# A float32 transformer block pair: activation transposes through DVE and a DRAM exchange in place of DVE blocks and PE

## The chip, the core and the metric

The kernel runs on one NeuronCore of one Trainium2 chip. The core has a matrix engine (PE), a vector engine (DVE), a scalar engine (ACT), a general engine (POOL) and a queue engine (SP) that here only issues DMA transfers. Each engine works through its own list of instructions in order and waits on semaphores for the others. Sixteen DMA engines move data between DRAM and the on-chip memory of 128 partitions; PE writes to a separate accumulator memory (PSUM), which DVE and ACT can read.

The metric is the device time of one execution in microseconds (us), the median of several runs. Lower is better.

## What is computed

Two transformer blocks over 256 tokens of width 2048, all in float32. Each ends in a gated FFN of hidden width 5632; these two FFNs are what the change touches most.

```python
def conv_ffn(h, w_up, conv_w, conv_b, w_down):          # block 1
    up = h @ w_up                                        # (256, 2048) @ (2048, 11264)
    padded = jnp.pad(up, ((0, 0), (CONV_WIDTH - 1, 0), (0, 0)))
    y = conv_b + conv_w[0] * padded[:, 0:seq]
    for tap in range(1, CONV_WIDTH):                     # three taps along the tokens
        y = y + conv_w[tap] * padded[:, tap:tap + seq]
    gate, val = jnp.split(y, 2, axis=-1)
    return (jax.nn.silu(gate) * val) @ w_down

def second_block(...):
    ...                                                  # two mixers, concatenated, @ w_out
    x = x + (jax.nn.silu(h2 @ w_gate) * (h2 @ w_up)) @ w_down
```

Ahead of its FFN, block 1 has a 16-head causal attention with forget gates, and block 2 has a gated linear attention (4 heads) beside a dilated attention (8 heads). Queries and keys are RMS-normalised by head in the two attentions; each block normalises its input by row, once before the mixer and once before the FFN.

## The kernel before

**Products.** All large products go through one routine, `gemm`. It makes an output of 256 tokens by 512 columns from activation tiles that have the contraction on their partitions ("turned" activations) and from weight blocks of 512 by 512 (1 MB, `raw`). To keep float32 accuracy on PE, ACT rounds each weight to a high part `wh` (line 105) and DVE takes the remainder `wl` (line 111); the activations are split in the same way, and PE adds three products (lines 118 to 120). A *unit* is half a weight block: 12 matmuls on one pair `wh`, `wl`. A gemm over 2048 rows has 8 units. The whole program has 784 units: first 12 gemms for q, k, v, then 4 (attention out), 22 of 8 units (first FFN, up), 4 of 22 units (first FFN, down), 12 (block 2 in), 4 (block 2 out), 22 (second FFN, gate and up), 4 of 22 units (second FFN, down).

**What sets the order.** The program is written in one fixed order, and each engine takes its own instructions from it in that order. Before the matmuls of unit u, `split_to(u + LEAD)` with LEAD = 4 writes out the split of unit u+4; there are 5 pairs of `wh`, `wl` (NSPL), so the split of unit u+4 can begin when PE has finished unit u-1. `dma_to` issues the load of a 1 MB block on SP, two blocks ahead of the split that reads it; there are 3 buffers (NRAW), so a load waits until DVE has split the block three before it. The work between the products (what a gemm's output needs) is written as Python generators. `pump()` runs each of them to its next `yield` after every unit but the last one of a gemm, so a `yield` puts what follows one unit later in every engine's list.

```python
for kg in kgs:
    while ready is not None and not ready(kg):
        pump()
    for half in range(2):
        split_to(u + LEAD)
        ...                       # 12 matmuls
        if n == tot:
            start_fast(evac(acc))
        else:
            pump()
```

**Turning activations.** A product leaves tokens on the partitions; the next product needs the contraction there. `flip` (line 296) does it on DVE with 16 transposes of 32 partitions by 256 elements, two to a pump, so that a flip spreads over 8 pumps; each instruction transposes its 32 by 32 blocks and moves them to another group of partitions. `transposes` (line 281) and line 656 do it on PE against an identity, into PSUM.

- `plain` flips q and k of head groups 0 to 2 of block 1, of both groups of the dilated attention, and of the linear attention. `head_norm` comes first (not in the linear attention): ACT squares, DVE sums, POOL makes the factor and multiplies. `attention` waits in Python until `kf` is there; its step s2 then puts the score matmuls `sc` into PE's list.
- `resid` flips three of the four column blocks of each residual.
- `conv_evac` serves the 22 gemms of the first FFN's up stage, pairs j = 0 to 10 of gate (part 0) and value (part 1). For j below PE_CONV = 8 it flips on DVE (tile `flip`); then ACT makes the current token's tap with the bias into `y` (line 664) and the two older taps into `taps` (line 667), POOL adds them (line 671). For j = 8 to 10 PE transposes (line 656, 4 to a group, 48 in all) and DVE adds the taps from PSUM. Part 0 ends with silu on ACT; in part 1 POOL multiplies by it (line 692), and ACT and DVE split the result into `g` for the down product.
- `up_evac` flips 10 of the 11 blocks of the second FFN on DVE and turns the last one with 8 transposes on PE.

Tiles between stages come from 33 slots that are given out in turn (`alloc`, `free`).

Of the kernel before, what the change touches and what calls it, by code (L numbers as in the profile page):

```python
# [40 lines left out]
PE_CONV = 8  # L41
# [3 lines left out]
def fox_gla_dilated_kernel(  # L45
# [29 lines left out]
    sidep = ctx.enter_context(tc.tile_pool(name="side", bufs=4, space=bass.MemoryType.PSUM))  # L75
    dramp = ctx.enter_context(tc.tile_pool(name="scratch", bufs=1, space=bass.MemoryType.DRAM))
# [23 lines left out]
    def col(c, n=1):  # L100
        return cols[:, c:c + n]
# [198 lines left out]
    def split_flipped(y, dst, gains):  # L300
        for half in range(2):
            d = dst[half]
            if gains is None:
                sl = slice(half * 2, half * 2 + 2)
                hi_of(d[:, :, 0], y[:, sl])
                lo_of(d[:, :, 1], y[:, sl], d[:, :, 0])
            else:
                for kk in range(2):
                    kt = half * 2 + kk
                    hi_of(d[:, kk, 0], y[:, kt], gains(kt))  # L310
                    lo_of(d[:, kk, 1], y[:, kt], d[:, kk, 0], gains(kt))

    def resid(cb, ss, tt, gcol, rname, done):
        def evac(acc):
# [4 lines left out]
            if cb < KG - 1:  # L319
                sumsq(ss, cb, h[cb])  # L320
                y = alloc([4, S], F32, "flip")
                yield from flip(h[cb], y)
                d = new_t(2, rname)
                split_flipped(y, d, gains)
                free(y)
# [37 lines left out]
    def plain(name, box, key, r, norm=False, flipped=False, gain=None):  # L363
        def evac(acc):
# [112 lines left out]
    def run_all():  # L477
# [156 lines left out]
        def conv_evac(j, part, keep):  # L634
            cb = part * JF + j

            def evac(acc):
                y = alloc([4, S], F32, "y")
                on_pe = j >= PE_CONV
                u_ = y.rearrange("p a c -> p (a c)").rearrange("p (t c) -> p t c", t=2)  # L640
                for t in range(2):
                    if not on_pe:
                        act.activation(out=u_[:, t], in_=acc[t], func=AF.Copy, scale=rows["r2"][:, t:t + 1])
                        continue
                    act.activation(out=y[:, t::2], in_=acc[t].rearrange("p (a c) -> p a c", a=2), func=AF.Copy,
                                   scale=rows["r2"][:, t:t + 1])
                yield
                if not on_pe:
                    f = alloc([4, S], F32, "flip")
                    yield from flip(u_, f)  # L650
                for half in range(2):
                    if on_pe:
                        ps = side([2, S], "up")
                        for kk in range(2):
                            for t in range(2):
                                pe.transpose(ps[:, kk, t * P:(t + 1) * P], y[:, half * 2 + t, kk * P:(kk + 1) * P],
                                             ident)
                    else:
                        ps = f[:, half * 2:half * 2 + 2]
                    if not on_pe:  # L660
                        tp = alloc([2, 2, S], F32, "taps")
                        for kk in range(2):
                            ch = cb * 4 + half * 2 + kk
                            act.activation(out=y[:, half * 2 + kk], in_=ps[:, kk], func=AF.Identity,  # L664
                                           scale=col(C_CW + 176 + ch), bias=col(C_CB + ch))
                            for d in (1, 2):
                                act.activation(out=tp[:, d - 1, kk, 0:S - d], in_=ps[:, kk, 0:S - d], func=AF.Copy,  # L667
                                               scale=col(C_CW + 176 - 88 * d + ch))
                        for d in (1, 2):
                            yy = y[:, half * 2:half * 2 + 2, d:S]  # L670
                            pool.tensor_tensor(out=yy, in0=yy, in1=tp[:, d - 1, :, 0:S - d], op=ALU.add)  # L671
                        free(tp)
                        yield
                        continue
                    for kk in range(2):
                        ch = cb * 4 + half * 2 + kk
                        yy = y[:, half * 2 + kk]
                        act.activation(out=yy, in_=ps[:, kk], func=AF.Identity, scale=col(C_CW + 176 + ch),
                                       bias=col(C_CB + ch))
# [5 lines left out]
                if not on_pe:  # L685
                    free(f)
# [375 lines left out]
```

## Time and profile before

| | |
|---|---|
| median of 3 runs | 2244.41 us (2244.35 to 2244.52) |
| the profiled execution, its own time | 2244.25 us |
| span of its instructions | 2242.5 us |
| PE busy | 2229.8 us, 99% |
| DVE busy | 1494.0 us, 67% |
| ACT busy | 1146.8 us, 51% |
| POOL busy | 259.7 us, 12% |
| DMA queue of SP, share of the 16 engines | 52.5%, 417.59 MB |

The span runs from the first to the last instruction; 1.75 us of the execution's time lie outside it. PE's busy time is the union of its matmuls, whose ends are modelled: a matmul is shown with 0.39 us though the next one starts 0.227 us after it. What PE loses is therefore read from the distance between starts and from its idle time, and not from the busy share alone.

### The profile page before, as it was taken

To read this page: it belongs to the slowest core of one execution; us is meant where nothing else is said; L and a number is where in the kernel's file an instruction comes from. 1 tells how busy PE (TensorE), PEld (TensorE's weight loads), DVE (VectorE), ACT (ScalarE), POOL (GpSimd) and SP (SyncE) were. 2 spreads that over 40 slices of the span, in tenths; PEclk is the share of its full clock that TensorE was granted. 3 is DMA by queue.
4 is the path that set the end of the run, shared out by engine and by line. 5 is a ranking of instruction groups with operands and counts; after the bars stand their busy time and mean duration, and the time that the engine had idled before them with its cause. 6 is when DMAs were issued, how large, how long until landed. Compare 5 with 4: busy or idle time off the path is not lost.

```text
span 2242.5 us, 25956 instructions
## 1 busy us (share of the span) xinstructions
PE 2229.8 (99%) x10004; PEld 1834.3 (82%) x10004; DVE 1494.0 (67%) x2012; ACT 1146.8 (51%) x1522; POOL 259.7 (12%) x210
## 2 busy tenths in 40 slices
PE   9999999999999999999999999999999999999999
PEld 7888888888888878888887887888888888888887
DVE  5877668777787776556666974586666666664443
ACT  6545554577667665444455544544444444443332
POOL 0323020033433310000111100000000000000000
PEclk9999999999999999999999999999999999999999
DMA  7654445545455554555554544555555555555553
GB/s 297 225 184 166 177 154 201 186 175 205 169 203 178 197 192 172 204 190 198 214 188 151 188 169 141 178 189 190 200 192 189 198 195 188 195 194 202 199 206 112
DMA packets 62189, 423.11 MB, mean 189 GB/s; under 512 B 6992, under 2 KB 7904, under 8 KB 12272
## 3 DMA queue, kind: packets, MB, share of 16 engines
q1 hardware_dynamic: 60272, 417.59, 52.5%
q0 software_dynamic: 928, 3.20, 0.4%
q8 instruction: 78, 1.28, 0.2%
q10 hardware_dynamic: 864, 0.66, 0.1%
q14 instruction: 47, 0.39, 0.0%
HBM read 419.30 MB, written 2.11 MB: 188 GB/s over the span
## 4 chain that ended last, share of the span: by engine, by line
PE 87%; DVE 5%; POOL 4%; ACT 2%; issue 1%; DMA 0%; ACTq 0%; DVEq 0%; SPq 0%
PE acc L118 28%; PE acc L119 28%; PE acc L120 28%; POOL y L671 3%; DVE wl L111 3%; DVE flip L296 1%; POOL y L692 1%; ACT taps L667 1%; ACT wh L105 0%; PE sc L413 0%; DMA xr<-in_x_t_dram 0%; PE pt L439 0%; PE nar L544 0%; ACT y L664 0%; DVE g L111 0%
## 5 line engine op out<-in xcount | busy, mean ns | idle before, releaser
L111 DVE TENSOR_TENSOR wl<-raw,wh 128x1024 fp32r<-128x1024 f32 (+1 forms) x786 | 973.8, 1243 | 598.6 <-ACT wh L105 593.9
L105 ACT CAST wh<-raw 128x1024 fp32r<-128x1024 f32 (+1 forms) x786 | 816.0, 1048 | 741.6 <-PE acc L120 726.7
L118 PE MATMUL acc<-wh,r 128*128 128x512 f32 x1792 | 703.1, 392 | 0.4 <-ACT wh L105 0.4
L119 PE MATMUL acc<-wl,r 128*128 128x512 f32 x1792 | 698.4, 390 | 4.1 <-DVE wl L111 4.1
L120 PE MATMUL acc<-wh,r 128*128 128x512 f32 x1792 | 697.9, 389 | 0.0
L119 PEld LDWEIGHTS acc<-wl,r 128*128 128x128 f32 x1792 | 336.6, 188 | 75.7 <-DVE wl L111 7.4
L118 PEld LDWEIGHTS acc<-wh,r 128*128 128x128 f32 x1792 | 336.5, 188 | 72.2 <-issue 2.5
L120 PEld LDWEIGHTS acc<-wh,r 128*128 128x128 f32 x1792 | 336.4, 188 | 70.2
L118 PE MATMUL acc<-wh,g 128*128 128x512 f32 x704 | 274.1, 389 | 0.0
L120 PE MATMUL acc<-wh,g 128*128 128x512 f32 x704 | 273.9, 389 | 0.0
L119 PE MATMUL acc<-wl,g 128*128 128x512 f32 x704 | 273.9, 389 | 0.0
L118 PE MATMUL acc<-wh,x 128*128 128x512 f32 x384 | 155.5, 405 | 0.2 <-ACT wh L105 0.2
L118 PEld LDWEIGHTS acc<-wh,g 128*128 128x128 f32 x704 | 132.2, 188 | 27.5
L119 PEld LDWEIGHTS acc<-wl,g 128*128 128x128 f32 x704 | 132.2, 188 | 27.3
L120 PEld LDWEIGHTS acc<-wh,g 128*128 128x128 f32 x704 | 132.1, 188 | 27.3
L119 PE MATMUL acc<-wl,x 128*128 128x512 f32 x384 | 149.8, 390 | 0.8 <-DVE wl L111 0.8
L120 PE MATMUL acc<-wh,x 128*128 128x512 f32 x384 | 150.0, 391 | 0.0
L671 POOL TENSOR_TENSOR y<-y,taps 128x510 f32<-128x510 f32 x64 | 106.4, 1662 | 253.5 <-ACT taps L667 250.1
L296 DVE STREAM_TRANSPOSE flip<-y 32x256 f32<-32x256 f32 x256 | 111.7, 436 | 5.6
L119 PEld LDWEIGHTS acc<-wl,x 128*128 128x128 f32 x384 | 72.2, 188 | 15.5 <-DVE wl L111 1.3
L120 PEld LDWEIGHTS acc<-wh,x 128*128 128x128 f32 x384 | 72.1, 188 | 15.6
L118 PEld LDWEIGHTS acc<-wh,x 128*128 128x128 f32 x384 | 72.2, 188 | 15.1 <-ACT wh L105 0.6
(206 smaller groups left out, 1611.8 us busy)
## 6 DMA issues: line engine op xcount, KB each, us to landing
raw<-in_w_dram SPq DMA_DIRECT2D x301, 1024.0 KB, 4.8
raw<-in_w7g_dram SPq DMA_DIRECT2D x44, 1024.0 KB, 4.8
raw<-in_w7u_dram SPq DMA_DIRECT2D x44, 1024.0 KB, 4.8
raw<-in_w_dram SPq DMA_DIRECT2D x4, 512.0 KB, 7.9
h<-in_x_dram SPq DMA_DIRECT2D x4, 512.0 KB, 9.5
ckb<-cum_dram POOLq DMA_DIRECT2D x4, 512.0 KB, 8.5
out_dram<-h SPq DMA_DIRECT2D x7, 256.0 KB, 2.2
xr<-in_x_t_dram SPq DMA_DIRECT2D x3, 512.0 KB, 8.0
```

The costliest lines, as they stand in the source:

```text
L105: act.copy(out_, in_)
L111: dve.tensor_tensor(out=out_, in0=in_, in1=hi.bitcast(F32), op=ALU.subtract)
L118: pe.matmul(out_, xh, wh, start=first, stop=False)
L119: pe.matmul(out_, xh, wl, start=False, stop=False)
L120: pe.matmul(out_, xl, wh, start=False, stop=last)
L296: dve.transpose(out=dv[32 * j:32 * j + 32, :, :, 32 * i:32 * i + 32], in_=sv[32 * i:32 * i + 32, :, :, j])
L667: act.activation(out=tp[:, d - 1, kk, 0:S - d], in_=ps[:, kk, 0:S - d], func=AF.Copy, scale=col(C_CW + 176 - 88 * d + ch))
L671: pool.tensor_tensor(out=yy, in0=yy, in1=tp[:, d - 1, :, 0:S - d], op=ALU.add)
L692: pool.tensor_tensor(out=y, in0=y, in1=sg, op=ALU.mult)
```

## The change

1. `flip` is now two DVE transposes of all 128 partitions by 512 elements (every 32 by 32 block is transposed where it stands, into a new tile `turn`), then a yield, then four DMA writes of 32 partitions each into a DRAM tile `way`, a yield, one DMA read of `way` back with the blocks at their final partitions, and two more yields. All five transfers are issued on SP. The read's target is the source tile itself (`into`) except in `resid`. What comes back has its tokens in four pieces by 32 for every 128 columns.
2. `ordered` puts the tokens in order: 4 copies on ACT of 128 by 256 (with the gain, where there is one). `split_flipped` uses it when there are gains, and otherwise splits straight from the pieces, 128 by 256 at a time.
3. `conv_evac` uses this for all 22 gemms: PE_CONV and the PE transposes of line 656 are gone. ACT makes the current tap from `n`, DVE adds the two older ones (8 instructions of 128 by 255 or 254), and DVE does the product with silu. POOL has no part in it.
4. `up_evac` uses it for the last block too, in place of 8 PE transposes.
5. A DRAM pool of 4 `way` tiles is added.

```diff
-    def flip(src, dst):
-        sv = src.rearrange("p t (k q c) -> p t k q c", q=4, c=32)
-        dv = dst.rearrange("p k (t r) -> p t k r", t=2)
+    def flip(src, into=None):
+        turn = alloc([4, S], F32, "turn")
+        sv = src.rearrange("p t (k q c) -> p t q k c", q=4, c=32)
+        qv = turn.rearrange("p q (k t r) -> p t q k r", t=2, r=32)
+        for t in range(2):
+            dve.transpose(out=qv[:, t], in_=sv[:, t])
+        yield
+        way = ways.tile([P, 4, S], F32, tag="way", name="way")
         for i in range(4):
-            for j in range(4):
-                dve.transpose(out=dv[32 * j:32 * j + 32, :, :, 32 * i:32 * i + 32], in_=sv[32 * i:32 * i + 32, :, :, j])
-                if j % 2:
-                    yield
+            nc.sync.dma_start(out=way[:, i].rearrange("(j c) e -> c j e", c=32), in_=turn[32 * i:32 * i + 32])
+        yield
+        held = alloc([4, S], F32, "flip") if into is None else into
+        f = held.rearrange("p a c -> p (a c)").rearrange("p (i e) -> p i e", i=4)
+        nc.sync.dma_start(out=f, in_=way)
+        yield
+        yield
+        free(turn)
+        return f.rearrange("p i (k t r) -> p k t i r", k=4, t=2), held
+
+    def ordered(f, name, scale=lambda kt: 1.0):
+        y = alloc([4, S], F32, name)
+        for kt in range(4):
+            act.activation(out=grid(y[:, kt]), in_=f[:, kt], func=AF.Copy, scale=scale(kt))
+        return y
...
@@ plain
-            y = alloc([4, S], F32, name + "f")
-            yield from flip(t_, y)
-            free(t_)
-            if gain is not None:
-                act.activation(out=y, in_=y, func=AF.Copy, scale=gain)
-            box[key + "f"] = y
+            f, held = yield from flip(t_, t_)
+            box[key + "f"] = ordered(f, name + "f", lambda kt: 1.0 if gain is None else gain)
+            free(held)
@@ conv_evac
+                u_ = alloc([2, 512], F32, "u")
+                for t in range(2):
+                    act.activation(out=u_[:, t], in_=acc[t], func=AF.Copy, scale=rows["r2"][:, t:t + 1])
+                yield
+                f, held = yield from flip(u_, u_)
+                n = ordered(f, "n")
+                free(held)
+                yield
                 y = alloc([4, S], F32, "y")
-                on_pe = j >= PE_CONV
...
+                for kt in range(4):
+                    ch = cb * 4 + kt
+                    act.activation(out=y[:, kt], in_=n[:, kt], func=AF.Identity, scale=col(C_CW + 176 + ch),
+                                   bias=col(C_CB + ch))
+                for kt in range(4):
+                    ch, yy = cb * 4 + kt, y[:, kt]
+                    for d in (1, 2):
+                        dve.scalar_tensor_tensor(out=yy[:, d:S], in0=n[:, kt, 0:S - d],
+                                                 scalar=col(C_CW + 176 - 88 * d + ch), in1=yy[:, d:S],
+                                                 op0=ALU.mult, op1=ALU.add)
+                    if kt == 1:
                         yield
...
-                pool.tensor_tensor(out=y, in0=y, in1=sg, op=ALU.mult)
+                dve.tensor_tensor(out=y, in0=y, in1=sg, op=ALU.mult)
@@ up_evac
-                if j < JF - 1:
-                    y = alloc([4, S], F32, "flip")
-                    yield from flip(t_, y)
-                    d = new_t(2, "g")
-                    split_flipped(y, d, None)
-                    free(y)
-                else:
-                    d = new_t(2, "g")
-                    transposes(t_, d, None)
+                f, held = yield from flip(t_, t_)
+                d = new_t(2, "g")
+                split_flipped(f, d, None)
+                free(held)
```

How the lists of three engines change. **SP**, from the early loads on, before (`raw` is a 1 MB weight block, `h` and `const` are loaded once):

```order
L154 DMA raw<-in_w_dram 128x2048
L163 DMA h_294<-in_x_dram 128x2x512
L154 DMA raw<-in_w_dram 128x2048
L159 DMA const<-in_const_dram 128x784
L154 DMA raw<-in_w_dram 128x2048 x251
```

and after the change, two gemms of the first FFN's up stage (`u` is the block being turned):

```order
L300 DMA way<-turn 32x4x256 x4
L154 DMA raw<-in_w_dram 128x2048
L304 DMA u<-way 128x1024
L154 DMA raw<-in_w_dram 128x2048 x3
L300 DMA way<-turn 32x4x256 x4
```

Of the four weight loads of a gemm, one now stands between the writes and the read that waits for them, and three behind that read.

**DVE**, the first FFN's up stage, before (`wl` is the weight split, `flip` the turned block, `g` the split of the finished one):

```order
L111 TENSOR_TENSOR g_4323<-y,g_4323 128x2x256
L111 TENSOR_TENSOR g_4326<-y,g_4326 128x2x256
L296 STREAM_TRANSPOSE flip<-y 32x2x4x32 x2
L111 TENSOR_TENSOR wl<-raw,wh 128x1024
L296 STREAM_TRANSPOSE flip<-y 32x2x4x32 x2
L111 TENSOR_TENSOR wl<-raw,wh 128x1024 x2
L296 STREAM_TRANSPOSE flip<-y 32x2x4x32 x4
```

and after it (L671 adds a tap, L683 is the product with silu, `turn` the new tile):

```order
L671 SCALAR_TENSOR_TENSOR y<-n,cols,y 128x254
L111 TENSOR_TENSOR wl<-raw,wh 128x1024 x2
L683 TENSOR_TENSOR y<-y 128x1024
L296 STREAM_TRANSPOSE turn<-u 128x16x32 x2
L111 TENSOR_TENSOR wl<-raw,wh 128x1024
L111 TENSOR_TENSOR g_5572<-y,g_5572 128x2x256
L111 TENSOR_TENSOR g_5575<-y,g_5575 128x2x256
L111 TENSOR_TENSOR wl<-raw,wh 128x1024 x4
L671 SCALAR_TENSOR_TENSOR y<-n,cols,y 128x255
```

The short transposes between the weight splits (two or four at a time, 16 to a gemm) have become one pair of long ones; five splits follow it before DVE needs what came back, and the taps (four, a split, four) and the product are new on DVE.

**ACT**, head group 1 of block 1, from k's output on, before (`pb` is the softmax, whose first row follows the score matmuls of PE):

```order
L369 ACTIVATE k<-acc_980,rsr_463 128x512
L369 ACTIVATE k<-acc_981,rsr_463 128x512
L355 ACTIVATE sq<-k 128x1024
L105 CAST wh<-raw 128x1024
L105 CAST o_554<-ov 128x256
L105 CAST wh<-raw 128x1024 x3
L381 ACTIVATE qf<-qf,gqk 128x1024
L105 CAST wh<-raw 128x1024 x4
L369 ACTIVATE v<-acc_1184,rsr_463 128x512
L369 ACTIVATE v<-acc_1185,rsr_463 128x512
L105 CAST wh<-raw 128x1024 x4
L425 ACTIVATE pb,st<-pb,st 128x128
```

and after it:

```order
L389 ACTIVATE k<-acc_999,rsr_465 128x512
L389 ACTIVATE k<-acc_1000,rsr_465 128x512
L375 ACTIVATE sq<-k 128x1024
L105 CAST wh<-raw 128x1024 x7
L316 ACTIVATE kf<-k 128x256 x4
L442 ACTIVATE pb,st<-pb,st 128x128
```

Before, DVE made `kf` and the softmax came after k's output and v's; now ACT's four copies from the DMA's target stand right before the softmax, seven weight splits after k's output, and PE's score matmuls of the same pump read them.

## Rows read from the trace of the kernel before

**Rows 1.** page: span; part 1, busy us (share) x instructions; part 2, PE clock

```profile
span 2242.5 us, 25956 instructions
PE 2229.8 (99%) x10004; PEld 1834.3 (82%) x10004; DVE 1494.0 (67%) x2012; ACT 1146.8 (51%) x1522; POOL 259.7 (12%) x210
...
PEclk9999999999999999999999999999999999999999
```

**Rows 2.** waits of PE, whole run: engine line <- releaser: us in total, times, longest

```profile
PE acc L119 <- DVE wl L111: 4.8, 7, 0.8
...
PE sc L412 <- DVE kf L296: 0.5, 1, 0.5
```

**Rows 3.** timeline of PE: start us, us, engine, line, operation, out<-in, count

```profile
394.34 0.39 PE L118 MATMUL acc<-wh,r 128*128 128x512 f32 x1
...
887.08 0.39 PE L118 MATMUL acc<-wh,g 128*128 128x512 f32 x1
...
1518.12 0.39 PE L118 MATMUL acc<-wh,r 128*128 128x512 f32 x1
...
1997.73 0.39 PE L118 MATMUL acc<-wh,g 128*128 128x512 f32 x1
```

**Rows 4.** waits from 580 to 810 us, in the first FFN's up stage

```profile
ACT y L664 <- DVE flip L296: 29.6, 8, 4.0
...
ACT g L105 <- POOL y L692: 21.8, 5, 4.8
...
ACT wh L105 <- PE acc L120: 0.2, 1, 0.2
```

**Rows 5.** waits from 1529 to 2008 us, in the second FFN's up stage

```profile
ACT wh L105 <- PE acc L120: 246.8, 153, 1.7
```

**Rows 6.** timeline of ACT and of DVE: one half block of weights is split

```profile
1995.21 1.05 ACT L105 CAST wh<-raw 128x1024 fp32r<-128x1024 f32 x1 [1.67 <-PE acc L120]
...
1996.30 1.23 DVE L111 TENSOR_TENSOR wl<-raw,wh 128x1024 fp32r<-128x1024 f32 x1 [1.50 <-ACT wh L105]
```

**Rows 7.** timeline of PE around four and around eight transposes

```profile
774.58 0.39 PE L120 MATMUL acc<-wh,r 128*128 128x512 f32 x1
774.81 0.60 PE L656 MATMUL up<-const,y 128*128 128x128 f32 x4
...
775.49 0.39 PE L119 MATMUL acc<-wl,r 128*128 128x512 f32 x1
...
2000.23 0.40 PE L120 MATMUL acc<-wh,g 128*128 128x512 f32 x1
2000.46 1.03 PE L281 MATMUL tp<-const,sg 128*128 128x128 f32 x8
...
2001.57 0.39 PE L119 MATMUL acc<-wl,g 128*128 128x512 f32 x1
```

**Rows 8.** groups by shape: xcount | busy us, mean ns | idle before

```profile
L296 DVE STREAM_TRANSPOSE flip<-y 32x256 f32<-32x256 f32 x256 | 111.7, 436 | 5.6
...
L680 DVE SCALAR_TENSOR_TENSOR y<-up,cols,y 128x255 f32<-128x255 f32 x24 | 11.5, 481 | 13.6 <-ACT y L678 13.5
...
L664 ACT ACTIVATE y<-flip,cols 128x256 f32<-128x256 f32 x64 | 38.0, 594 | 41.7 <-DVE flip L296 41.5
```

**Rows 9.** DMA issues: out<-in engine op x count, KB each, median us to landing

```profile
raw<-in_w_dram SPq DMA_DIRECT2D x301, 1024.0 KB, 4.8
...
ckb<-cum_dram POOLq DMA_DIRECT2D x4, 512.0 KB, 8.5
out_dram<-h SPq DMA_DIRECT2D x7, 256.0 KB, 2.2
...
rel<-in_rel_dram POOLq DMA_DIRECT2D x2, 512.0 KB, 5.6
```

**Rows 10.** timeline of PE and of POOL after the k product of head group 1

```profile
131.43 0.39 PE L118 MATMUL acc<-wh,x 128*128 128x512 f32 x1
...
137.72 2.39 POOL L361 TENSOR_TENSOR k<-k,rsh 128x1024 f32<-128x1024 f32 x1
```

More of the change, by code (lines that the diff above doesn't have):

```diff
@@ L40 @@
 WARM = 4
-PE_CONV = 8
 @with_exitstack
@@ L75, in fox_gla_dilated_kernel @@
     sidep = ctx.enter_context(tc.tile_pool(name="side", bufs=4, space=bass.MemoryType.PSUM))
+    ways = ctx.enter_context(tc.tile_pool(name="ways", bufs=4, space=bass.MemoryType.DRAM))
     dramp = ctx.enter_context(tc.tile_pool(name="scratch", bufs=1, space=bass.MemoryType.DRAM))
@@ new lines, in grid, with split_flipped @@
+    def grid(ap):
+        return ap.rearrange("p (t i r) -> p t i r", t=2, i=4)
+    def ordered(f, name, scale=lambda kt: 1.0):
[3 more added lines that the diff above has]
+        return y
+    def split_flipped(f, dst, gains):
+        if gains is None:
+            for kt in range(4):
+                d = dst[kt // 2]
+                hi, lo = grid(d[:, kt % 2, 0]), grid(d[:, kt % 2, 1])
+                hi_of(hi, f[:, kt])
+                lo_of(lo, f[:, kt], hi)
+            return
+        y = ordered(f, "y", gains)
+        for half in range(2):
+            d, sl = dst[half], slice(half * 2, half * 2 + 2)
+            hi_of(d[:, :, 0], y[:, sl])
+            lo_of(d[:, :, 1], y[:, sl], d[:, :, 0])
+        free(y)
@@ L320, in evac @@
                 sumsq(ss, cb, h[cb])
-                y = alloc([4, S], F32, "flip")
-                yield from flip(h[cb], y)
+                f, held = yield from flip(h[cb])
                 d = new_t(2, rname)
-                split_flipped(y, d, gains)
-                free(y)
+                split_flipped(f, d, gains)
+                free(held)
                 tt.extend(d)
@@ L637, in evac @@
             def evac(acc):
-                y = alloc([4, S], F32, "y")
-                on_pe = j >= PE_CONV
[L640 to L646, printed above, removed]
@@ L647, in evac @@
-                yield
[L648 to L679, printed above, removed]
-                        dve.scalar_tensor_tensor(out=yy[:, 1:S], in0=ps[:, kk, 0:S - 1], scalar=col(C_CW + 88 + ch),
-                                                 in1=yy[:, 1:S], op0=ALU.mult, op1=ALU.add)
-                        dve.scalar_tensor_tensor(out=yy[:, 2:S], in0=ps[:, kk, 0:S - 2], scalar=col(C_CW + ch),
-                                                 in1=yy[:, 2:S], op0=ALU.mult, op1=ALU.add)
-                    yield
@@ new lines, in evac @@
+                for kt in range(4):
+                    ch, yy = cb * 4 + kt, y[:, kt]
[4 more added lines that the diff above has]
+                    if kt == 1:
+                        yield
+                free(n)
+                yield
@@ L948, in evac @@
                 yield
[L949 to L957 removed]
+                f, held = yield from flip(t_, t_)
+                d = new_t(2, "g")
+                split_flipped(f, d, None)
+                free(held)
                 gt2[2 * j], gt2[2 * j + 1] = d
[L959 removed]
             return evac
```

16 lines of the change are left out of this document (removed).

## The prediction

> **What bounds the kernel now.** I read the page first. PE is busy 2229.8 of 2242.5 us and its clock is at full in every slice [rows 1], so only two things can shorten this kernel: matmuls that go away, and the little that PE waits. The list of waits names the second: seven times PE stood for DVE's weight remainder, 4.8 us in all, and once 0.5 us for `kf` [rows 2]. To size both I compared two stages that should cost PE the same. The up stages of the two FFNs are each 22 gemms of 8 units, 2112 matmuls, with 8 transposes of the last residual block. From first matmul to first matmul of the next stage, the first takes 887.08 - 394.34 = 492.7 us, the second 1997.73 - 1518.12 = 479.6 us [rows 3]. The second is as fast as PE goes: starts lie 0.227 us apart (11 steps from 1997.73 to 2000.23 [rows 3, 7]), and 2112 x 0.227 = 479.4. So the first stage loses 13.1 us.
>
> Where? Ten of the twelve groups of four transposes lie in it. A group takes 775.49 - 774.58 = 0.91 us over what would be two steps, 0.45, so it costs 0.46 [rows 7]; ten are 4.6 us. The other 8.5 us are waits and the late steps around them. Their source is the lead of the splits. In the second stage ACT begins a split when PE gives a buffer free, and DVE ends it 2.3 us later (1995.21 to 1997.53 [rows 6]); PE reads it four units, 4 x 12 x 0.227 = 10.9 us, after its start, so the lead is 8.6 us, and there ACT waited 153 times for PE [rows 5]. Between 580 and 810 us of the first stage it did so once: ACT's list stood 29.6 us for `flip` on DVE and 21.8 us for POOL's product [rows 4], the splits behind those waits came late, and the lead was gone.
>
> **The change part by part.**
>
> *PE.* 48 + 8 transposes go. The eight in the second FFN cost 2001.57 - 2000.23 - 0.45 = 0.89 us [rows 7]. Two groups of the first FFN lie behind its up stage: 0.92 us.
>
> [...]
>
> *DVE.* A transpose of 32 by 256 takes 436 ns [rows 8]. Of 128 by 512 no row shows one. Low bound: it costs by its length as other DVE work on 128 partitions, where 1024 elements take 1.23 us [rows 6], so half of that and a little, 0.7 us. High bound: the four quadrants one after the other, 8 x 436 = 3.5 us. I take 0.7: 436 ns for 256 elements is close to the 481 ns that a tap of 255 takes on all 128 partitions [rows 8], so the quadrants seem to matter little. For a pair of gemms (43.5 us of PE) DVE then has 16 splits x 1.23 = 19.7, four transposes 2.8, 16 taps x 0.481 = 7.7 [rows 8], the product 1.2 and the split of `g` 1.4: 32.8 us. Before: 19.7 + 32 x 0.436 + 1.4 = 35.1. With the high bound it would be 44.0, just over PE.
>
> *ACT.* 16 x 1.05 [rows 6], 4 copies of u at 0.7 (half of a split and a little), 8 `ordered` copies and 8 current taps at no more than 0.594 [rows 8], silu 1.1, `g` 1.3: 31.5 us of 43.5. Before it had 16 older taps in place of the 8 copies.
>
> *POOL's* product and adds were in ACT's way [rows 4]; they go.
>
> *SP and the exchange.* Each of the 54 flips (12 for q and k, 9 in the residuals, 22, 11) now sends 0.5 MB out and back, 57 MB on top of 417.59; by bytes the 52.5% of the DMA engines become 60%. SP issues the writes when the transposes are done, then one weight load, then stands until the writes have landed, and issues the read; the next weight load queues behind. How long does a trip take? Writes: 256 KB to DRAM landed in 2.2 us [rows 9]; I use that for each of the four, which start 0.3 us apart. Read: 512 KB landed in 5.6 us beside the weights, 8.5 us after a DRAM write; a whole 1 MB block takes 4.8 [rows 9]. Low 4.4 (a share of the 4.8 behind the block ahead), high 8.5; I take 5 to 5.6.
>
> In the up stage, counted from the end of a gemm: u is ready at 0.7, the split ahead is done at 3.0, the transposes at 4.4, the last write is out at 5.7 and landed at 7.9, the read lands at 12.3 to 16.4, mostly 13. ACT comes to the copies five splits later, when the fifth unit has begun and its split is done, at 4 x 2.72 + 1.05 = 11.9. It waits 0.4 to 4.5 us against a lead of 8.6 us, and with 31.5 of 43.5 us of work it makes this up before the next gemm. So I cost the exchange at nothing in both FFNs: the lead hides it. The weight block behind the read is issued at about 8, while its buffer comes free only at 3 x 2.72 + 2.3 = 10.5, so it isn't late either. The first stage then runs like the second: 13.1 us back.
>
> *Heads.* The cover is thin in one place. `kf` of the five flipped attention groups is made by ACT's copies in the same pump in which PE gets `sc`, seven units after k's gemm: PE is there 7 x 2.72 = 19.0 us after it. In group 1, POOL has k normalised at 140.11, 8.7 us after 131.43 [rows 10]. Transposes to 10.1, writes out at 11.4, landed 13.6, read landed at 18.0, 19.2 or 22.1 (4.4, 5.6, 8.5), first copy 0.5 us more. PE waits 0, 0.7 or 3.6 us. Five times that is 0, 3.3 or 18 us; I take 2.0 us, nearest to the first two because on SP's own queue only one block stands ahead. Queued behind the waiting `sc` is all of PE. The old wait for `kf`, 0.5 us, goes into this.
>
> *The rest.* Residual flips are done three to five pumps before a gemm needs them; the second FFN's last block has 20 units before it is read. Both at nothing.
>
> Sum against the profiled execution: 13.1 + 0.9 + 0.9 - 2.0 = 12.9 us; the span becomes 2229.6, with the 1.75 us outside it 2231.35. The median stood 0.16 us over that execution: **2231.5 us**.
>
> **Rivals.**
>
> *A: the round trip is late for `kf`.* For it: a DRAM write followed by a read is in the trace only as 8.5 us for the read. Against: that read repeats 16 KB over all partitions. At 3.6 us and more a group it takes 18 us back and the time is 2244.4 - 14.9 + 18 = 2247.5; at half of that, 2238.5. Chance 0.15, about half of it at 2241 or below.
>
> *B: the transposes leave PE but the lead isn't restored,* because the long transposes cost the high bound or ACT's new waits for the read take the place of those for DVE and POOL. Then only the transposes are saved, 4.6 + 0.9 + 0.9 = 6.4, less 2.0: 2240. For it: ACT had 51 us of such waits in 230 us [rows 4]. Against: work on no engine passes 33 of 43.5 us. Chance 0.08.
>
> *C, slower: the exchange outlasts the lead.* ACT works in order, so a read that lands late holds every later split. With about 2.4 us of lead used by the four copies themselves (4 x 0.594 [rows 8]), PE stands once ACT waits over 6 us, that is when write and read together pass 12.3 us (I count 7 to 8; the slowest rows make 2.2 + 8.5 = 10.7 [rows 9]). From there each us costs 33 us, one for each flip of the two FFNs: at 13 us, 2231 + 23 = 2254; at 14, 2287. For it: five more transfers per gemm in one queue, in which SP stands for landings. Against: the queue is only half full. Chance 0.07.
>
> [...]
>
> *Without effect* can't be on PE: its list after the change no longer has line 656 or the last eight transposes. What could undo it are A to C.
>
> **How the numbers follow.** Forecast 2229 to 2234: 0.66. A 0.15, B 0.08, C 0.07; 0.04 for less than 2229, with nothing waiting for `kf` and something gained in the head stage. The range 2229 to 2241 holds the forecast, half of A and most of B: 0.80. A run tells from no change what is over 0.2%, 4.5 us. Faster by that: 0.66 + 0.04 + 0.07 of A + 0.05 of B = 0.82; within it 0.09 (the rest of A and B); slower 0.09 (C, 0.02 of A).
>
> **What would show it.** Right: the first up stage takes 479 to 481 us; ACT's splits there wait for PE as in the second; the new transposes take about 0.7 us; `way` lands in 2 to 3 us and the read in 4 to 6; PE waits for ACT at `sc` by no more than 1 us, five times at most. Wrong: reads over 8 us, PE waits at `wh` or `wl` in either FFN, transposes of 3 us, or SP's loads landing late for ACT.

## The result, and the profile after

The changed kernel is slower: 2265.8 us, median of 5 runs (2264.71 to 2268.96), against 2244.41 us for the kernel before (2244.24 to 2246.13); ratio 1.0095, 95% interval 1.0081 to 1.011. The forecast was 2231.5, with 2229 to 2241 as its range; both were wrong, and so was the sign. The profiled execution took 2266.26 us, 1.76 us of it outside its span.

The page of the changed kernel (span; busy us, share and instructions; PE clock by slice; SP's DMA queue), against [rows 1]:

```profile
span 2264.5 us, 25811 instructions
PE 2235.4 (99%) x9948; PEld 1829.2 (81%) x9948; DVE 1275.7 (56%) x1511; ACT 1141.7 (50%) x1565; POOL 115.6 (5%) x135
...
PEclk9899999999999999999999999999999999999999
...
q1 hardware_dynamic: 99152, 474.23, 60.6%
```

The work moved as foreseen: DVE 218 us less, POOL 144 less, ACT 5 less, 57 MB more on the queue. PE has 56 instructions less and is nevertheless busy longer, with a slice of lower clock near the start. The waits of PE in the whole run, against [rows 2]:

```profile
PE sc L429 <- ACT kf L316: 19.1, 5, 6.5
PE acc L119 <- DVE wl L111: 4.5, 9, 0.8
```

The five waits for `kf` that the prediction put at 0.4 us each are 3.8 us each on average. The stage starts, against [rows 3]:

```profile
405.94 0.39 PE L118 MATMUL acc<-wh,r 128*128 128x512 f32 x1
...
897.63 0.39 PE L118 MATMUL acc<-wh,g 128*128 128x512 f32 x1
...
1541.38 0.39 PE L118 MATMUL acc<-wh,r 128*128 128x512 f32 x1
...
2020.99 0.39 PE L118 MATMUL acc<-wh,g 128*128 128x512 f32 x1
```

The first up stage takes 897.63 - 405.94 = 491.7 us, where 479.6 was forecast; it was 492.7. The second takes 479.6, as before. The first began 11.6 us later than before, so the other loss begins ahead of it. Cut at the first matmul of the units in question, in the same way, the two stretches in which the five flipped head groups of the attentions make their scores (units 16 to 72 and 392 to 440) took 314.5 us together and now take 340.0. The sum of what changed: heads +25.4, first up stage -1.0, first down stage +1.2, all the rest -3.0 (0.9 of it the eight transposes of the second FFN, 0.7 the first 16 units): 22.6 us between the first and the last unit; the spans differ by 22.0.

**Heads.** PE at the first score matmuls of group 0, and the granted clock there (columns of the second: stretch, length, busy PE, PEld, DVE, ACT, POOL, clock, DMA share, GB/s):

```profile
83.87 0.80 PE L429 MATMUL sc<-kf,qf 128*128 128x128 f32 x2 [6.49 <-ACT kf L316]
...
84.96 0.99 PE L118 MATMUL acc<-wh,x 128*128 128x512 f32 x1
```
```profile
76.00:84.00 8.00, 1.51 (x8) 0.93 (x6) 2.36 (x2) 2.96 (x6) 3.30 (x10) 0.76 0.93 378
84.00:87.00 3.00, 3.00 (x9) 2.46 (x9) 0.64 (x4) 2.97 (x9) 1.98 (x7) 0.51 0.82 339
87.00:90.00 3.00, 3.00 (x15) 2.45 (x14) 1.94 (x4) 2.51 (x5) 0.00 (x0) 1.00 0.06 22
```

PE stands 6.49 us, and for the 3 us after that its clock is granted at 0.51: 9 matmuls in 3 us instead of 15. The 3 us behind the first dilated group's wait of 3.85 us, and behind the 2.30 us of group 2:

```profile
1206.65:1209.65 3.00, 3.00 (x8) 2.53 (x9) 0.64 (x4) 2.97 (x8) 0.00 (x0) 0.50 0.03 14
235.20:238.20 3.00, 3.00 (x15) 2.53 (x16) 1.24 (x7) 2.46 (x8) 0.00 (x0) 1.00 0.18 76
```

The clock was low behind the three longest waits (0.51, 0.50 and 0.50 behind 6.5, 4.2 and 3.8 us) and full behind the two of 2.3 (1.00). So the long waits cost more here than their length: the five make 19.1 us, the stages lost 25.4. By the counts of matmuls, three times 3 us at the low clock cost some 4 of the other 6.3 us (an estimate); the rest I did not follow.

One trip, that of group 1 (`k` normalised on POOL, transposes, writes, read, copies; in the first row PE goes on from k's gemm, in the last it makes the scores):

```profile
138.78 0.39 PE L118 MATMUL acc<-wh,x 128*128 128x512 f32 x1
...
145.87 2.62 POOL L381 TENSOR_TENSOR k<-k,rsh 128x1024 f32<-128x1024 f32 x1
148.52 1.31 DVE L296 STREAM_TRANSPOSE turn<-k 128x512 f32<-128x512 f32 x2 [1.79 <-POOL k L381]
149.85 1.79 SPq L300 DMA_DIRECT2D way<-turn  x4
...
154.37 0.34 SPq L304 DMA_DIRECT2D k<-way  x1
...
159.77 1.33 ACT L316 ACTIVATE kf<-k 128x256 f32<-128x256 f32 x4 [3.42 <-DMA k<-way]
160.24 0.49 PE L429 MATMUL sc<-kf,qf 128*128 128x128 f32 x2 [2.26 <-ACT kf L316]
```

Counted from 138.78, `k` is ready at 9.7 us, the transposes end at 11.0, the last write is issued at 12.9, the read at 15.6, the copies start at 21.0 and the scores at 21.5. PE is there at 19.0, after seven units.

**First up stage.** Waits from 405.9 to 897.6 us, against [rows 4]:

```profile
ACT n L316 <- DMA u<-way: 122.7, 20, 7.8
ACT wh L105 <- PE acc L120: 30.7, 23, 1.7
```

The waits for DVE's flips and POOL's product are gone, and ACT stands for the read instead, in 20 of the 22 gemms and 6.1 us on average. The new operations cost what was said (groups by shape; DMA issues with KB each and us to landing):

```profile
L296 DVE STREAM_TRANSPOSE turn<-u 128x512 f32<-128x512 f32 x44 | 28.5, 687 | 0.0
```
```profile
way<-turn SPq DMA_DIRECT2D x216, 128.0 KB, 2.6
u<-way SPq DMA_DIRECT2D x22, 512.0 KB, 5.5
```

### The profile page after: what moved, and what is told of

It is laid out like the page before. It is cut to its first block, busy times and chain, and to the rows that moved or that the text cites. A ratio compares the mean times of both kernels' runs of the same rounds, so it can differ in the third digit from the quotient of the medians.

```text
span 2264.5 us, 25811 instructions
## 1 busy us (share of the span) xinstructions
PE 2235.4 (99%) x9948; PEld 1829.2 (81%) x9948; DVE 1275.7 (56%) x1511; ACT 1141.7 (50%) x1565; POOL 115.6 (5%) x135
## 3 DMA queue, kind: packets, MB, share of 16 engines
q1 hardware_dynamic: 99152, 474.23, 60.6%
## 5 line engine op out<-in xcount | busy, mean ns | idle before, releaser
L111 DVE TENSOR_TENSOR wl<-raw,wh 128x1024 fp32r<-128x1024 f32 (+1 forms) x786 | 956.4, 1227 | 821.8 <-ACT wh L105 821.5
L316 ACT ACTIVATE n<-u 128x256 f32<-128x256 f32 x88 | 29.5, 406 | 136.2 <-DMA u<-way 136.2
L119 PEld LDWEIGHTS acc<-wl,x 128*128 128x128 f32 x384 | 72.5, 189 | 15.6 <-DVE wl L111 1.3
L671 DVE SCALAR_TENSOR_TENSOR y<-n,cols,y 128x255 f32<-128x255 f32 (+1 forms) x176 | 81.0, 481 | 3.1
```

What stands on the lines that cost most here:

```text
L111: dve.tensor_tensor(out=out_, in0=in_, in1=hi.bitcast(F32), op=ALU.subtract)
L119: pe.matmul(out_, xh, wl, start=False, stop=False)
L316: act.activation(out=grid(y[:, kt]), in_=f[:, kt], func=AF.Copy, scale=scale(kt))
L671: dve.scalar_tensor_tensor(out=yy[:, d:S], in0=n[:, kt, 0:S - d], scalar=col(C_CW + 176 - 88 * d + ch), in1=yy[:, d:S], op0=ALU.mult, op1= ...
```

## The experiments

My theory after this reading: all of the loss is time in which something stood for the round trip; the copies of `ordered` and the scores are in the lists before the read can have landed. Rivals: the added traffic disturbs the weights; the trip is long because it stands behind weight loads; DVE and ACT simply have too much to do. Stage times below are taken from PE's starts, as above.

| kernel | heads | first up | first down | median us |
|---|---|---|---|---|
| before | 314.5 | 492.7 | 240.3 | 2244.4 |
| changed | 340.0 | 491.7 | 241.5 | 2265.8 |
| no trip (e8) | 315.0 | 479.6 | 239.4 | 2228.5 |
| trip made, not read (e9) | 315.0 | 479.6 | 239.4 | 2228.1 |
| heads by old flip (e5) | 314.3 | 485.4 | 241.4 | 2235.5 |
| FFN copies 2 steps later (e2) | 341.9 | 479.6 | 239.4 | 2253.1 |
| head copies 2 steps later (e3) | 313.7 | 486.8 | 241.6 | 2236.3 |
| both later (e1) | 313.9 | 479.6 | 239.4 | 2228.7 |
| old flip in heads, FFN later (e6) | 314.5 | 479.6 | 239.7 | 2229.0 |
| trip on POOL's queue (e4) | 375.9 | 569.2 | 248.6 | 2401.2 |

### Without the exchange; with it, but nobody waiting

```diff
@@ e8: flip
-        (the four writes to way, the read of way)
+        return turn.rearrange("p i (k t r) -> p k t i r", k=4, t=2), turn
@@ e9: flip, all five transfers stay
-        free(turn)
-        return f.rearrange("p i (k t r) -> p k t i r", k=4, t=2), held
+        free(held)
+        return turn.rearrange("p i (k t r) -> p k t i r", k=4, t=2), turn
```

> The block exchange through DRAM is left out (neither the four writes nor the read), and the in-order copies read the result of the two stream transposes directly, so what follows works on data in the wrong order; all work on the engines stays as it is in the changed kernel. Latency theory (all that the change lost, it lost while something stood waiting for the read): the head stages give back the 25.4 us that they lost, the first FFN up stage falls from 491.7 to about 479.6 us, the sum is 2265.8 - 25.4 - 12.1 = about 2228 us. Work theory (eight taps and the product on VectorE and six copies on ScalarE are too much for the first FFN, whatever the trip does): the up stage stays at 490 to 492 us and only the heads gain, about 2240 us.

> The four writes and the read are made as in the changed kernel, but the in-order copies read the result of the stream transposes and not what the read brings, so nothing waits for the read; the data are in the wrong order. Latency theory: as without the trip, about 2228 us, the up stage about 480. Contention theory (474 MB on the queues instead of fewer, and reads that push the weight stream back): PE or the splits wait for weights, the time stays several us above the run without the trip; if it is the whole of the cost in the first FFN, the up stage stays near 491.

Measured: 2228.5 us (ratio 0.9929, 0.9906 to 0.9951) and 2228.1 us (0.9929, 0.9907 to 0.9952). All that the change lost, and all that it was to bring, hangs on waiting for the read. The traffic itself costs nothing that shows: in e9 SP's queue carries the same 474.23 MB. The work on DVE and ACT alone, without the waits, costs nothing either.

### The two places apart

```diff
@@ e5: plain (heads) back to the 16 small transposes
-            f, held = yield from flip(t_, t_)
-            box[key + "f"] = ordered(f, name + "f", ...)
+            y = alloc([4, S], F32, name + "f")
+            yield from flip_dve(t_, y)
...
@@ e2: conv_evac; and in flip, free(turn) right behind the read
                 f, held = yield from flip(u_, u_)
+                for _ in range(2 if j < 8 else 0):
+                    yield
                 n = ordered(f, "n")
```

> Only the q and k transposes of the head stages go back to the sixteen small VectorE transposes of the kernel before; residuals and both FFNs stay as in the changed kernel. If the head stages' loss is the trip in front of the scores alone: 2265.8 - 25.4 = about 2240.4 us, the first FFN unchanged at 491 to 492. If the loss in the heads comes from elsewhere (the splits' lead, the queue): above 2250.

> In the first eight of eleven FFN blocks of each half the in-order copies stand two steps of the schedule later (about 5.5 us); the buffer of the transposed blocks comes free as soon as the writes have read it. If ScalarE's wait for the read (7.8 us at 22 gemms, 6.2 us on average) is what keeps the splits without lead: the first FFN up stage falls from 491.7 to 480 to 484 us, the time to 2254 to 2258. If the work on VectorE and ScalarE itself is too much, or what is late is VectorE: 490 to 492, 2264 to 2268.

Measured: 2235.5 us (0.9968, 0.9947 to 0.9989) and 2253.1 us (1.0036, 1.0016 to 1.0056). The heads gave back all that they had lost, and the up stage, though its code was the same, another 6.3. In e2 the up stage runs at PE's pace, the forecast's 479.6; the heads keep their loss. The 33 slots do not suffice to hold all eleven blocks of each half longer; in e2 the first eight are.

### Both repaired

```diff
@@ e3: plain (heads); e1 is e2 and e3 together; e6 is e5 and e2 together
             f, held = yield from flip(t_, t_)
+            for _ in range(2):
+                yield
             box[key + "f"] = ordered(...)
```

> Only the copies of q and k two steps later (the scores with them). Place theory: the head stages give back 20 to 25 us, the first FFN stage falls at most to the 485 that it showed with the old heads: 2235 to 2246. Theory that the trip is too slow by itself (it grows as the weight loads move with it): 2258 or more.

> The whole changed kernel, with in-order copies two steps later for the FFN blocks and for q and k; since the scores start once the copies of k are in the list, they too move two steps (5.4 us) later on TensorE. If only the place is wrong and not the trip: 2253.1 with later FFN copies, less 20 to 25 of the head stages, about 2228 to 2234 us; what may stay is the first group, where the read beside the four 512 KB loads lands 7.8 us behind TensorE. If scores that stand later push the rest of the attention into the next group: 2240 or more.

> Heads by the sixteen small VectorE transposes of the kernel before, residuals and FFN blocks by the round trip, the FFN's in-order copies two steps later in the first eight blocks of each half. If the two losses are apart and add up: 2235.5 with only the heads put back, less 5.8 (first FFN up stage 485.4 to 479.6) and 2.0 (down stage 241.4 to 239.4) = about 2227.7 us, 0.75 % faster than the kernel before. If the later place only helps when the heads are late, or slots of the buffer pool hold the next block up: 2233 to 2236.

Measured: e3 2236.3 us (0.9966, 0.9951 to 0.9981), e1 **2228.7 us** (0.9931, 0.9916 to 0.9946), e6 2229.0 us (0.9935, 0.9918 to 0.9951). e1 is the change as it was meant, all transposes by the exchange, and beats the kernel before, 2244.0 us beside it, by 15.4 us; it is as fast as the kernel without a trip. The waits of PE in e1, whole run, without a warm-up at the start:

```profile
PE acc L119 <- DVE wl L111: 1.0, 2, 0.8
```

So the trip need not be shorter. It needs places that are as far behind it as it is long.

### Another queue

```diff
-            nc.sync.dma_start(out=way[:, i]...
+            nc.gpsimd.dma_start(out=way[:, i]...
-        nc.sync.dma_start(out=f, in_=way)
+        nc.gpsimd.dma_start(out=f, in_=way)
```

> The writes and the read of the trip are issued by GpSimd on its own queue, so they no longer stand behind SyncE's 1 MB weight loads; all else as in the changed kernel. If standing behind the weights is most of the trip's length (write packets began 1.5 us late, the read was mixed with a weight load): ScalarE's wait of 6.2 us at a gemm of the first FFN falls to 2 to 4, the scores wait 2 to 5 us less, 2245 to 2257 us; the first group of heads may get worse, since the four 512 KB loads stand on that queue. If the 16 DMA engines are shared whatever the queue: 2263 to 2268.

Measured: 2401.2 us (1.0701, 1.0679 to 1.0722). Both expectations fall. Landing times, and one trip in the first up stage (POOL issues, ACT copies):

```profile
way<-turn POOLq DMA_DIRECT2D x216, 128.0 KB, 6.0
u<-way POOLq DMA_DIRECT2D x22, 512.0 KB, 3.7
```
```profile
490.55 1.30 DVE L296 STREAM_TRANSPOSE turn<-u 128x512 f32<-128x512 f32 x2
...
492.14 2.19 POOL L300 DMA_DIRECT2D way<-turn  x4 [17.17 <-DVE turn L296]
500.88 0.56 POOL L304 DMA_DIRECT2D u<-way  x1 [6.55 <-DMA way<-turn]
...
504.48 1.34 ACT L316 ACTIVATE n<-u 128x256 f32<-128x256 f32 x4 [8.98 <-DMA u<-way]
```

The read of `u` lands sooner from POOL's queue than from SP's (3.7 us against 5.5, medians of 22), but the writes land after 6.0 us instead of 2.6 (medians of 216). From transposes to copies the trip takes 13.9 us here; on SP's queue it took 10.7 to 12.9. ACT stood 225.0 us for the 22 reads, against 136.2 in the changed kernel. Meanwhile SP issued two weight loads beside these writes:

```profile
493.02 2.60 SPq L154 DMA_DIRECT2D raw<-in_w_dram  x2
```

On SP's queue the next weight load was issued behind the four writes (in the changed kernel at 501.56 us, behind writes issued from 499.51 to 501.46). Here the two overlap, and POOL, done with issuing the writes at 494.33 us, stood 6.55 us for the last of them to land. Whether the writes land late because of these loads, no run tests.

### How late was the trip, and whose doing was it

```diff
@@ e10: flip (the slot edit of e2 alone)
         nc.sync.dma_start(out=f, in_=way)
+        free(turn)
@@ e11: as e2, range(1 if j < 8 else 0)
@@ e12: as e1, one yield in plain
```

> The changed kernel with one bookkeeping edit that the later-copies kernels also have: the slot of the transposed block is given back right after the read is issued, two steps earlier; the copies stay where they are. If that edit has no part in the gain of the later copies: 2263 to 2268 us, first FFN up stage 490 to 492. If it has, below 2260.

> Copies of the first eight FFN blocks of each half one step (2.7 us) later, not two. Balance theory: in the changed kernel the lead of the splits falls by about 1.4 us at each gemm, since ScalarE's work and its wait of 6.2 us take longer than the 21.8 us of a gemm; a wait shorter by 2.7 turns that round, the lead holds: stage 479.6 to 482, about 2253 to 2256 us, nearly all that two steps gave (2253.1). If the whole wait must be covered: the stage about halfway, 485 to 488, 2258 to 2262.

> As the kernel with all copies two steps later, but those of q and k (and with them the scores) only one step, 2.7 us. Place theory, from how late the copies of k were in the changed kernel (2 us at groups 1 and 2, 3.5 at the first dilated group, 7.8 at group 0): one step covers groups 1 and 2, leaves about 1 at the first dilated group and 5 at group 0: 2228.7 + 6 = 2233 to 2236 us. If the lateness moves along with the place (because loads move too): 2245 or more; if one step is as good as two: 2228 to 2230.

Measured: e10 2261.2 us (1.0079, 1.005 to 1.0108), e11 2256.0 us (1.0049, 1.0012 to 1.0086), e12 2230.95 us (0.9943, 0.9921 to 0.9966). In e11 the up stage is at 479.6: one step was enough. e10 was a miss: its up stage took 486.0, and the slots seemed to have a part. e12 was better than I said: one more `yield` moved the first scores of group 0 from behind 23 units to behind 25 (two, in e1, to behind 26), since no pump runs after the last unit of a gemm. That is 5.4 us on PE, not 2.7, and it covers even group 0 but for 1.0 us.

The balance that I used for e11 did not hold: ACT was busy 284.7 of the 491.7 us, so even 122.7 us of waiting left it room. The changed kernel's up stage (columns as above):

```profile
405.90:897.60 491.70, 488.38 (x2121) 394.60 (x2121) 322.58 (x412) 284.65 (x414) 0.89 (x2) 1.00 0.67 230
```

So what made each gemm later than the one ahead? I followed it in the changed kernel from gemm to gemm, counted from the end of the gemm:

| gemm | transposes start | copies start | transposes to copies | copies to next transposes |
|---|---|---|---|---|
| 1 | 3.0 | 13.8 | 10.8 | 11.0 |
| 2 | 3.0 | 14.1 | 11.1 | 11.8 |
| 3 | 4.1 | 15.5 | 11.4 | 10.5 |
| 4 | 4.3 | 17.0 | 12.7 | 11.7 |
| 5 | 6.9 | 18.4 | 11.5 | 10.5 |
| 9 | 10.6 | 21.4 | 10.8 | 10.5 |
| 13 | 12.0 | 22.9 | 10.9 | 10.5 |

The trip does not get longer. It starts later and later, until the lead is gone, and the way from the copies to the next transposes is nearly rigid: 10.5 us, or 11.7 where the product stands in it. The changed kernel, gemm 3 to 4 (DVE's, SP's and ACT's rows in order of time):

```profile
487.66 1.34 ACT L316 ACTIVATE n<-u 128x256 f32<-128x256 f32 x4 [3.37 <-DMA u<-way]
...
489.97 1.23 DVE L111 TENSOR_TENSOR wl<-raw,wh 128x1024 fp32r<-128x1024 f32 x1 [4.42 <-ACT wh L105]
491.12 1.91 DVE L671 SCALAR_TENSOR_TENSOR y<-n,cols,y 128x255 f32<-128x255 f32 x4
492.94 1.22 DVE L111 TENSOR_TENSOR wl<-raw,wh 128x1024 fp32r<-128x1024 f32 x1
493.72 1.25 ACT L657 ACTIVATE u<-acc,rsr 128x512 f32<-128x512 f32 x2
494.08 1.91 DVE L671 SCALAR_TENSOR_TENSOR y<-n,cols,y 128x255 f32<-128x255 f32 x4
495.91 2.36 DVE L111 TENSOR_TENSOR wl<-raw,wh 128x1024 fp32r<-128x1024 f32 x2
498.18 1.30 DVE L296 STREAM_TRANSPOSE turn<-u 128x512 f32<-128x512 f32 x2
...
499.51 1.95 SPq L300 DMA_DIRECT2D way<-turn  x4
501.56 0.38 SPq L154 DMA_DIRECT2D raw<-in_w_dram  x1
504.14 0.34 SPq L304 DMA_DIRECT2D u<-way  x1
...
510.85 1.34 ACT L316 ACTIVATE n<-u 128x256 f32<-128x256 f32 x4 [4.84 <-DMA u<-way]
```

It is a closed chain: each round of it starts with the end of the round before. ACT's copies wait for the read; the splits behind them wait on ACT; DVE's taps need the copies; the next block's transposes stand in DVE's list behind those splits and taps, though they need none of them (u was ready at 493.72 + 1.25 = 495.0); the next writes, the next read and the next copies follow. From copies to copies 510.85 - 487.66 = 23.2 us, and 22.1 to 23.2 for the three rounds ahead of the fifth gemm, while PE needs 21.76 for a gemm. The lead pays for the difference for nine gemms; then PE runs at the chain's pace, 22.7 us a gemm from the tenth on.

### The chain tested

```diff
@@ e13: the changed kernel, conv_evac, one step, slots as they were
+                for _ in range(1 if j < 8 else 0):
+                    yield
                 n = ordered(f, "n")
@@ e14: the changed kernel, both transposes of a conv block made twice
-    def flip(src, into=None):
+    def flip(src, into=None, times=1):
...
-        for t in range(2):
+        for t in list(range(2)) * times:
             dve.transpose(out=qv[:, t], in_=sv[:, t])
...
-                f, held = yield from flip(u_, u_)
+                f, held = yield from flip(u_, u_, 2)
@@ e15: e13 and e14 together
```

> The changed kernel with a single edit: the copies of the first eight FFN blocks of each half stand one step later; slots are given back as in the changed kernel. It parts the later place from the earlier slot, which came together so far (one step with the earlier slot: up stage 479.6 us; the earlier slot alone: 486.1). If the place of the copies is what feeds the lateness back: up stage 479.6 to 481, 2252 to 2256 us. If the earlier slot was half of it: 484 to 487, 2257 to 2261.

Measured: 2253.5 us (1.0042, 1.0027 to 1.0057), up stage 479.6. The place alone does it. The product, which in every second gemm stood ahead of the next transposes, and one split now stand behind them (DVE's and ACT's rows of one gemm):

```profile
513.92 1.34 ACT L316 ACTIVATE n<-u 128x256 f32<-128x256 f32 x4 [1.30 <-DMA u<-way]
...
524.30 1.30 DVE L296 STREAM_TRANSPOSE turn<-u 128x512 f32<-128x512 f32 x2
525.52 1.18 DVE L111 TENSOR_TENSOR wl<-raw,wh 128x1024 fp32r<-128x1024 f32 x1
526.63 1.22 DVE L685 TENSOR_TENSOR y<-y 128x1024 f32<-128x1024 f32 x1
...
535.05 1.34 ACT L316 ACTIVATE n<-u 128x256 f32<-128x256 f32 x4 [0.68 <-DMA u<-way]
```

This round is 535.05 - 513.92 = 21.1 us, under 21.76. With the wait for the read (38.3 us in 20 gemms, the longest 7.3) it varies, from 21.1 to 23.0 in the gemms with the later place; but a longer trip is followed by a shorter way to the next transposes, down to 10.3 us, so the lateness does not add up. The transposes stay 4.8 us behind their gemm from the second gemm to the sixteenth, the last with the later place, and slide again in the six behind it, which have the old one (9.5 at the 21st).

> The changed kernel, in which the two stream transposes of each block of the first FFN's up stage are made twice (same source, same target): 1.3 us more of VectorE at each of 22 gemms, nothing else. Chain theory (from the copies of one block to those of the next 22.1 to 23.2 us, against 21.76 of a gemm): the chain becomes 23.4 to 24.5, the lead is gone after about 5 gemms and not 9, and each later gemm takes some 2.1 us more than PE needs: 17 x 2.1 = 36, the up stage about 515 us, the time 2283 to 2295. Load theory (VectorE is busy 323 of 492 us and has room for 29 more): the stage 490 to 494, 2264 to 2270.

> The same doubling in the kernel whose copies stand one step later (there the chain takes 21.1 us, 0.6 less than a gemm, and the up stage 479.6). Chain theory: the chain becomes 22.4, each gemm comes 0.6 later than the one before, the lead of 8 to 9 us lasts about 14 gemms: up stage 481 to 488 us, 2254 to 2262. Load theory: 479.6 as without the doubling, 2252 to 2255.

Measured: e14 2278.0 us (1.015, 1.0121 to 1.018), up stage 503.0; e15 2270.9 us (1.0118, 1.0063 to 1.0173), up stage 488.4. The second pairs are 24 us of DVE work in e14 (346.8 us busy in the stage for 322.6), on an engine that idled 169 of the 491.7 us of that stage. They cost 11.4 and 8.8 us of the stage. So DVE's load as such is not the bound, and a longer round costs time though DVE idles a third of the stage. e15 is the clearest: the transposes slide from 4.8 to 10.4 us behind the gemm in ten gemms, some 0.6 us each as expected, where without the doubling they stood still. The size was missed for e14 (515 expected): the lead lasted for seven gemms and not five, and from the eighth on a gemm took 23.3 us on average, 1.6 more than PE needs and not 2.1. In the changed kernel it took 22.7 from the tenth on, so of about 1.1 us more of DVE work in a round only 0.6 reached PE; from transposes to copies a round took 12.2 us for 11.7. Why not all of it, I did not follow: the direction of the chain is shown, its length is not a plain sum. e15's profile also lost 6.7 us in the head stages and 4.4 in the rest, against e13, which the doubling does not touch. The mean granted clock of its profiled run was 0.993, that of e13's 0.996; why, I can't explain.

**Left open:** why the up stage takes 485 to 487 us in e3, e5 and e10 and 491.7 in the changed kernel, where the FFN's copies have the same place. In all of them the lead runs out, after the 9th gemm in the changed kernel and after the 16th in e5; what sets how fast, I did not isolate.

## Why the prediction was wrong

The forecast was 34.3 us too low: 23.4 of that in the heads, 12.1 in the first up stage and 2.1 in the first down stage, while 3.3 us came off elsewhere, which the sum did not hold.

- **Prices of the new operations: right.** Transposes 0.69 us for 0.7; writes landed after 2.6 for 2.2, reads after 5.5 for 5 to 5.6; the queue at 60.6% for 60. The last term of 0.9, the eight transposes of the second FFN, came as it was.
- **The exchange hidden by the lead, the 13.1 us: the step that failed in the FFN.** Its single trip was nearly right: copies "mostly 13" us behind the gemm, and 13.8 in the first. What failed is the sentence that ACT "makes this up before the next gemm", drawn from 31.5 us of work in 43.5. I compared loads with time, and never asked what the next trip's start stands behind. That start stands in DVE's list behind the splits and taps that wait, by way of ACT, for the trip before. By the fourth gemm the copies were at 17.0, by the ninth at 21.4. 12.1 of the 13.1 us stayed away. The term of 0.9 in the down stage came as +1.2, because the lead was gone when that stage began: its first twelve units took 2.2 us more than PE needs, and in e1 nothing.
- **The heads, -2.0: right mechanism, wrong size, and the larger part of the miss.** The term measured 25.4 us. The bounds for one group, 0 to 3.6 us, held for groups 1 and 2, which waited 2.3 each. Every step of group 1's trip came later than laid out: `k` ready at 9.7 us for 8.7, the last write issued at 12.9 for 11.4 (four issues took 1.8 us, not 4 x 0.3), the read issued at 15.6 for 13.6. But group 0 waited 6.5, with four loads of 512 KB on POOL's queue beside its read, and the two dilated groups 3.8 and 4.2, all three beyond the upper bound: one group's rows had been taken for all five. On top lay the matmuls at the clock of 0.50 to 0.51, behind three of the waits. I chose the value near the low end on the ground that only one block stands ahead on SP's queue; the upper end was in the sum, with its 18 us.
- **What I saw and did not weigh:** the shorter generator of the new flip lets the scores come earlier. Before, group 0's first scores stood behind 28 units, now behind 23: 13.6 us of cover had gone with the yields. I priced the trip against the new place, and did not say that the place was free to choose.
- **The rivals.** A (18 us back) and B (the lead not restored, because ACT's waits for the read take the others' place) both came true at once, in the words that I had given them. I had added their chances as if one excluded the other; both rest on the length of one trip. Taken together at their prices they give 2244.4 - 6.4 + 18 = 2256 us, still 10 short. In A's grounds, each of the reads that took 8.5 us repeats 4 KB over all partitions; 16 KB is all four. C's rule, that PE stands once the trip passes some length, was near: its threshold of a 6 us wait of ACT is where the waits ended up (6.1 on average), but the price per us came from the chain, and each gemm paid only what the chain was longer than PE.
- **The 56 transposes off PE: right as such.** Of the kernels that leave nothing out, e1 and e6, both without them, are the fastest (2228.7 and 2229.0 us); the loss came from the wait for the trip.

## What to carry to other kernels

Price a long transfer against the place of whoever waits for it, and count in the schedule how many steps that place is behind; when a change replaces many short steps by a few, its consumers move up too (here by five units). Then close the chain: if the next round's first instruction stands, in any engine's list, behind the last of this round, add up one whole round and compare it with the period of the engine that bounds. If it is longer, idle time on the other engines is no cover, and moving four copies by one step can be worth nearly as much as the whole change was to bring (12.3 us here, of 12.9).

## What the runs showed of the hardware beside this

- The same writes, 128 KB from 32 partitions to DRAM in runs of 1 KB, landed after 2.6 us from SP's queue and after 6.0 from POOL's (medians of 216, beside the weight loads); each issue occupied POOL for 0.56 us (119.2 us for 216). Against the kernel before, the 56.6 MB of writes and reads added 27648 packets of 512 B to 2 KB and 6912 of 2 to 8 KB on SP's queue; from POOL's they added none of the first kind and 13824 of the second, 4 KB each on average. The 512 KB read of a block of the first FFN landed sooner from POOL's queue, 3.7 against 5.5 us, though the same weights were then spread over a stage of 569 us instead of 492; that of `k` did too (3.7 against 5.3), those of `q`, of the second FFN and of the residuals did not (5.4 against 5.4, 4.9 against 4.8, 4.8 against 4.7).
- In the changed kernel, behind waits of 6.5, 3.8 and 4.2 us without a matmul PE's clock was granted at 0.50 to 0.51 of full for 3 us of work; behind the two of 2.3 us it stayed full.
- 57 MB more in a queue that was busy 52.5% cost no time that shows as long as nothing waited for them (e9 2228.1 us, e8 without them 2228.5).
